# An encoder's gated MLP: the first contraction of 18 of 24 tile pairs by seven half products, the second in five pieces

## The chip, the cores and the metric

The kernel runs on one core of one Trainium2 chip. The metric is the device time of one execution in microseconds (us). Three runs of the kernel before took 1204.39, 1204.51 and 1204.84 us; their median is 1204.51 us.

## The reference

Two layers (L = 2) work on x of 512 tokens by 1024 features, in float32. Each layer has a mixing part (neighbourhood attention beside a recurrent branch) and a gated MLP; a last RMSNorm follows. The change works on the MLP:

```python
h = rmsnorm(x, g_ffn[l])
u = h @ w_up[l]                                  # 1024 -> 6144
u_act, u_lin = jnp.split(u, 2, axis=-1)
u_act = depthwise_conv(u_act, conv_ffn_w[l], conv_ffn_b[l], (1, 1))
x = x + (jax.nn.gelu(u_act, approximate=True) * u_lin) @ w_down[l]   # 3072 -> 1024
```

So tile j of the 24 tiles (128 features each) of `u_act` meets tile 24 + j of `u_lin`: these two are the *pair* j, and their product, tile j of h, is contracted with `w_down`.

## The kernel before, in words

Activations lie transposed: 128 features on the partitions, 512 tokens along the free axis. The tokens are stored in an order in which eight rows of a 64-wide grid alternate; `natural` and `by_row` (L350 on) are views that undo it for the convolution.

**Precision.** TensorE multiplies float32r values. Every operand is split into a high part (ScalarE copies to float32r) and a low part (VectorE subtracts), and `mm3` (L242 to L245) issues three matmuls per 128x128 block: high by high, high by low, low by high. All matmuls of the MLP but those at the very end have 512 columns, a whole PSUM bank.

**Weights.** `weight_plan` lists chunks of 128x1024 (eight blocks) in the order of their use. `load_to` (L170) starts their loads on SP's queue into two buffers `raw`, at most six chunks ahead; `split_to` (L190) makes the high and low part at most three chunks ahead (L157), on ScalarE (L205) and VectorE (L206), into four buffers each. `chunk` hands one out. The weights of layer 1's mixing are split during layer 0's MLP by `split_later` (L212): loads and stores of both parts on GpSimd's queue, the split at L222 and L223. In layer 1 they are loaded again as `kept`.

**MLP.** The first group (L866 to L873) computes pairs 0 and 1 in four banks, k by k, as the normalised inputs `xg` appear; before its k = 6 PE forms the sum of squares over the features (`columns`, tile `fcps`), before k = 7 it spreads the reciprocal root over the partitions (`rows`, tile `g_ffn_rb`). From then on each pair takes two columns of eight blocks (tiles `pa`, `pl`; L874 to L877), 48 matmuls. `mlp_tile` (L843 to L857) scales by `rbf`, does the three-tap convolution (L848 to L851), GELU on ScalarE (L853), the product with the linear tile (L854) and the split of h (L367, L368). After pairs 0 to 11 the second contraction takes its first twelve k blocks: four output tiles at once in four banks, then four one by one (tiles `dn`, L894 to L911); after pairs 12 to 23 the other twelve. `summed` (L882) scales the result and adds it to x. In layer 1 the last two output tiles are computed in token halves of 256 columns (`finish`, L435 to L506, tiles `dnf`), so that the final RMSNorm of the first half runs beside the products of the second.

**Order.** The framework orders each engine's instructions when the program is built; those emitted under `urgent()` (L151) go ahead of others that are ready. At run time each engine executes its list in order, and a waiting instruction holds all behind it.

## Time and profile before

| what | value |
|---|---|
| median of three runs | 1204.51 us |
| the profiled execution | 1204.35 us |
| span of its instructions | 1202.6 us |
| PE, weight loads, VectorE, ScalarE, GpSimd busy | 1188.4, 992.1, 752.9, 511.7, 114.0 us |
| mean granted clock of TensorE | 0.996 of full speed |
| layer 0: mixing, MLP | 0 to 204, 204 to 598 us |
| layer 1: mixing, MLP | 598 to 797, 797 to 1190 us |
| bytes over the DMA queues | 151.86 MB |

The profiled execution is 1.75 us longer than its span, and 0.16 us shorter than the median. Busy time is the time in which at least one instruction of that engine is executing: a matmul's record is longer than the step from one matmul to the next, so for PE the starts are read, not the durations.

### The profile page before, as it was taken

How to read it: one execution, taken by the hardware profiler on the slowest of the kernel's cores; microseconds unless marked ns; L12 is line 12 of the kernel's file. 1: busy time of each engine (PE TensorE's matmuls, PEld its weight loads, DVE VectorE, ACT ScalarE, POOL GpSimd, SP SyncE). 2: the span in 40 equal slices, each digit the busy share in tenths (PEclk: the TensorE clock that was granted, in tenths of full speed). 3: DMA queues.
4: the chain of work that ended last, by engine and by line, in shares of the span. 5: the costliest groups of instructions: out<-in, count | busy, mean ns of one | idle time of the engine just before them, and what ended most of it. 6: DMA issues, size and time to landing. Idle time of an engine off the chain costs nothing.

```text
span 1202.6 us, 14575 instructions
## 1 busy us (share of the span) xinstructions
PE 1188.4 (99%) x5534; PEld 992.1 (83%) x5534; DVE 752.9 (63%) x1226; ACT 511.7 (43%) x753; POOL 114.0 (9%) x230
## 2 busy tenths in 40 slices
PE   9999999999999999999999999999999999999996
PEld 8878888888888888888888888888888888888886
DVE  7988967776644567653736679587555336565443
ACT  6668854434321334422408578354233213333231
POOL 1102110123210122200002012000000000000000
PEclk9999999999999999999999999999999999999998
DMA  7222214376643376733256442232323232323222
GB/s 237 82 87 89 82 38 139 106 237 236 221 164 103 134 231 215 237 115 104 88 176 200 130 159 71 62 112 90 98 96 104 90 105 88 104 89 105 88 70 70
DMA packets 51046, 151.86 MB, mean 126 GB/s; under 512 B 6432, under 2 KB 9632, under 8 KB 50976
## 3 DMA queue, kind: packets, MB, share of 16 engines
q1 hardware_dynamic: 41792, 122.21, 31.1%
q0 software_dynamic: 8640, 28.32, 7.2%
q8 instruction: 43, 0.70, 0.2%
q10 hardware_dynamic: 544, 0.40, 0.1%
q14 instruction: 27, 0.22, 0.1%
HBM read 129.93 MB, written 20.97 MB: 125 GB/s over the span
## 4 chain that ended last, share of the span: by engine, by line
PE 91%; ACT 4%; DVE 3%; issue 1%; DVEq 0%; POOLq 0%; POOL 0%; ACTq 0%
PE dn L243 7%; PE dn L245 7%; PE dn L244 7%; PE pl L243 7%; PE pa L243 7%; PE pa L244 7%; PE pl L244 7%; PE pa L245 7%; PE pl L245 7%; PE out L245 2%; PE out L243 2%; PE out L244 2%; PE s L690 1%; PE xr L243 1%; PE up L243 1%; PE xr L244 1%
## 5 line engine op out<-in xcount | busy, mean ns | idle before, releaser
L205 ACT ACTIVATE hi<-raw 128x1024 fp32r<-128x1024 f32 (+1 forms) x189 | 197.6, 1046 | 380.5 <-PE dn L244 154.3
L206 DVE TENSOR_TENSOR lo<-raw,hi 128x1024 fp32r<-128x1024 f32 (+1 forms) x189 | 227.8, 1206 | 134.7 <-ACT hi L205 133.3
L845 DVE TENSOR_TENSOR ua<-pa,g_ffn_rb 128x512 f32<-128x512 f32 x44 | 30.4, 692 | 104.5 <-PE pa L245 104.5
L853 ACT ACTIVATE uc<-uc,cols 128x512 f32<-128x512 f32 x48 | 34.8, 724 | 116.2 <-DVE uc L851 116.1
L854 DVE TENSOR_TENSOR ua<-pl,uc 128x512 f32<-128x512 f32 x44 | 30.3, 689 | 45.0 <-PE pl L245 43.4
L467 POOL TENSOR_TENSOR fin_r<-fin_ms,expo 128x2 f32<-128x2 f32 x2 | 1.4, 696 | 377.0 <-DVE fin_ms L465 377.0
L851 DVE SCALAR_TENSOR_TENSOR uc<-ua,cols,uc 128x511 f32<-128x511 f32 x48 | 36.0, 751 | 1.6
L228 POOL DMA_DIRECT2D kept<-lhi x36 | 19.5, 542 | 182.1 <-ACT lhi L222 180.2
L849 DVE SCALAR_TENSOR_TENSOR uc<-ua,cols,uc 128x511 f32<-128x511 f32 x48 | 35.8, 746 | 0.1
L705 ACT ACTIVATE prob<-prob,mx 128x192 f32<-128x192 f32 (+1 forms) x64 | 27.5, 431 | 16.1 <-DVE mx L703 16.0
L223 DVE TENSOR_TENSOR llo<-lraw,lhi 128x512 fp32r<-128x512 f32 x36 | 24.7, 688 | 13.9 <-ACT lhi L222 13.9
L818 DVE TENSOR_TENSOR dns<-dn,g_ffn_rb 128x512 f32<-128x512 f32 x24 | 16.3, 689 | 24.8 <-PE dn L245 24.8
L222 ACT ACTIVATE lhi<-lraw 128x512 fp32r<-128x512 f32 x36 | 22.1, 616 | 8.0 <-DMA lraw<-in_w 8.0
L245 PE MATMUL out<-atth,lo 128*128 128x512 f32 x64 | 25.4, 397 | 0.0
L244 PE MATMUL out<-attl,hi 128*128 128x512 f32 x64 | 25.1, 394 | 0.0
L243 PE MATMUL out<-atth,hi 128*128 128x512 f32 x64 | 24.9, 402 | 0.0
L848 DVE TENSOR_SCALAR uc<-ua,cols 128x512 f32<-128x512 f32 x48 | 23.4, 488 | 1.5
L228 POOL DMA_DIRECT2D kept<-llo x36 | 19.5, 542 | 45.9 <-DVE llo L223 42.8
L690 PE MATMUL s<-k,q_pair 128*128 128x192 f32 (+1 forms) x128 | 22.7, 317 | 0.1
L640 POOL CAST edge<-vh 64x128 fp32r<-64x128 f32 x24 | 9.5, 394 | 120.3 <-ACT vh L627 55.9
L698 DVE CUSTOM_DVE_ANT_0 prob<-s,bias 128x192 f32<-128x192 f32 (+1 forms) x64 | 18.3, 337 | 3.9 <-PE s L690 3.6
L690 PEld LDWEIGHTS s<-k,q_pair 128*128 128x128 f32 x128 | 19.8, 190 | 1.0 <-DVE k L604 0.8
(935 smaller groups left out, 3633.6 us busy)
## 6 DMA issues: line engine op xcount, KB each, us to landing
raw<-in_w SPq DMA_DIRECT2D x183, 512.0 KB, 3.5
lraw<-in_w POOLq DMA_DIRECT2D x36, 256.0 KB, 4.6
kept<-lhi POOLq DMA_DIRECT2D x36, 256.0 KB, 2.5
kept<-llo POOLq DMA_DIRECT2D x36, 256.0 KB, 3.0
hi<-kept SPq DMA_DIRECT2D x36, 256.0 KB, 2.9
lo<-kept SPq DMA_DIRECT2D x36, 256.0 KB, 4.0
x<-in_x SPq DMA_DIRECT2D x8, 256.0 KB, 4.9
bias<-in_bias SPq DMA_DIRECT2D x8, 224.0 KB, 2.5
```

Of the source, the lines that this page charges most:

```text
L205: nc.scalar.activation(hi[:, sl], raw[:, sl], AF.Copy)
L206: nc.vector.tensor_tensor(out=lo[:, sl], in0=raw[:, sl], in1=f32(hi[:, sl]), op=ALU.subtract)
L228: nc.gpsimd.dma_start(d, f32(parts[h][n]))
L243: nc.tensor.matmul(ps, a[0], b[0], start=start, stop=False)
L244: nc.tensor.matmul(ps, a[0], b[1], start=False, stop=False)
L245: nc.tensor.matmul(ps, a[1], b[0], start=False, stop=stop)
L690: nc.tensor.matmul(ps[:, o:o + ROWS * w], q_pair[:, b], kt[:, ROWS * kc0:ROWS * (kc0 + w)], start=True, stop=True)
L845: nc.vector.tensor_tensor(out=by_row(ua), in0=natural(pa), in1=natural(rbf[0]), op=ALU.mult)
L849: nc.vector.scalar_tensor_tensor(out=c[:, 1:], in0=ua[:, :T - 1], scalar=w[0], in1=c[:, 1:], op0=ALU.mult, op1=ALU.add)
L851: nc.vector.scalar_tensor_tensor(out=c[:, :T - 1], in0=ua[:, 1:], scalar=w[2], in1=c[:, :T - 1], op0=ALU.mult, op1=ALU.add)
L853: nc.scalar.activation(c, c, AF.Gelu_apprx_tanh, bias=col("conv_ffn_b", j, l))
L854: nc.vector.tensor_tensor(out=natural(ua), in0=natural(pl_), in1=by_row(c), op=ALU.mult)
```

## The change

Only the MLP's pairs 6 to 23, the cut of the second contraction, the weight queue and some buffers change.

- **Seven products.** For a pair, split the contraction in two halves of four k blocks, the tokens in two halves of 256, and the outputs in their two tiles. Eight half products would give the pair; after sums of the weight halves and of the input halves, seven do. Each is 4 x 3 matmuls of 256 columns. Products 1, 6, 5, 3 accumulate in one bank, 7 and 4 in a second, 2 in a third; ScalarE copies the first bank after products 1, 6 and 5, and VectorE adds. `TURNS` orders the products of neighbouring pairs so that they alternate.
- **Weight sums.** `pair_sums` makes two summed chunks per pair on VectorE (four operations of 512), from up to six units ahead; the split then has 3.5 chunks per pair (parts a, b, c and the half part d) where there were two. Four `raw` buffers take the place of two; four new buffers `p_sum` hold the sums.
- **Inputs.** `operands` scales, sums and splits the inputs once per layer, for k = 0 to 3, during piece 0. Pairs 0 to 5 stay with eight products, in three groups.
- **After the products.** The linear tile is formed in halves, the convolution's first step moves to ScalarE, the scaling of the result falls away.
- **Second contraction** after pairs 0 to 5, 6 to 9, 10 to 13, 14 to 18 and 19 to 23.
- **Kept weights.** Only the low part is stored and reloaded, now on SP's queue; the high part is made again in layer 1. The zeroed tiles of the attention move into the `p_sum` buffers and are zeroed in each layer.

```diff
-HALF = NJ // 2
+PIECES = [0, 6, 10, 14, 19, NJ]
...
+FIRST_TURNS = [(0, 1), (0, 2), (1, 1), (0, 6), (1, 2), (0, 7), (0, 5), (1, 6), (0, 3), (1, 7), (0, 4), (1, 5)]
+TURNS = [(0, 1), (0, 2), (-1, 3), (0, 6), (0, 7), (-1, 4), (0, 5)]
+LAST_TURNS = [(0, 1), (0, 2), (-1, 3), (0, 6), (-1, 4), (0, 5), (0, 7), (0, 3)]
+PART = {1: ("a", 0), 2: ("a", 1), 6: ("b", 0), 7: ("b", 1), 5: ("c", 0), 3: ("c", 1), 4: ("d", 0)}
...
+    return [(j, m) for j in range(j0, j1) for m in range(4)] + [(j, m) for m in range(4, 8) for j in range(j0, j1)]
...
-    AHEAD_LOAD, AHEAD_SPLIT = 6, 3
+    AHEAD_LOAD, AHEAD_SUM, AHEAD_SPLIT = 7, 6, 3
...
+    def pair_sums(i):
+        a, b = raws[i], raws[i + 1]
+        s23 = p_sum.tile([P, 1024], F32, tag="sum", name=f"sb{i}")
+        s14 = p_sum.tile([P, 1024], F32, tag="sum", name=f"sc{i}")
+        lower, upper = slice(0, 512), slice(512, 1024)
+        for out, x0, x1, op in ((s14[:, lower], b[:, lower], b[:, upper], ALU.add),
+                                (s23[:, lower], s14[:, lower], a[:, lower], ALU.subtract),
+                                (s23[:, upper], a[:, lower], b[:, lower], ALU.subtract),
+                                (s14[:, upper], a[:, upper], s23[:, lower], ALU.subtract)):
+            with urgent(0):
+                nc.vector.tensor_tensor(out=out, in0=x0, in1=x1, op=op)
+        sums[i] = {"b": s23, "c": s14}
...
+                src = sums[i][part] if part in ("b", "c") else raws[i]
...
+    def split_later(split=True):
+        if not made:
+            if later:
+                i = later.pop(0)
+                raw = p_w2.tile([P, 1024], F32, tag="w2", name=f"lraw{i}")
+                nc.sync.dma_start(raw[:, 0:width(i)], w_d[i][:, 0:width(i)])
+                made.extend((i, raw))
...
+            kept[i] = p_kept.tile([P, width(i)], F32, tag=f"kept{i}", name=f"kept{i}")
+            nc.sync.dma_start(kept[i], raw[:, 0:width(i)])
+            made.clear()
...
-            nc.scalar.activation(probs_of[k // 4][:, k % 4], x[k][:, N:], AF.Copy, scale=col("g_final", k))
-        for m in (6, 7):
-            products(0, m, bank(0, m), 0, HALF)
-        ps = bank(1, 6)
-        products(1, 6, ps, 0, 5)
+        products(0, 6, bank(0, 6))
+        for k in range(5):
+            gained(k)
+        products(0, 7, bank(0, 7))
+        products(1, 6, bank(1, 6))
+        gained(5)
         r0 = columns(0)
-        products(1, 6, ps, 5, 9)
+        products(1, 7, bank(1, 7))
         rows(0, r0)
-        products(1, 6, ps, 9, HALF)
-        for k in range(6):
-            gained(k)
-        products(1, 7, bank(1, 7), 0, HALF)
         r1 = columns(1)
         for k in (6, 7):
             gained(k)
         rows(1, r1)
...
-            nc.vector.tensor_scalar(out=c, in0=ua, scalar1=w[1], scalar2=None, op0=ALU.mult)
+            nc.scalar.activation(c, ua, AF.Copy, scale=w[1])
...
+            for n in range(2):
+                cs = slice(n * N2, (n + 1) * N2)
+                nc.vector.tensor_tensor(out=natural(ua[:, cs]), in0=natural(lin[:, cs]), in1=by_row(c)[:, :, 4 * n:4 * n + 4],
+                                        op=ALU.mult)
+            hi = big(p_h, "h", f"h{l}_{j}h", F32R)
+            lo = big(p_h, "h", f"h{l}_{j}l", F32R)
+            behind(nc.scalar.activation(hi, ua, AF.Copy), first)
+            nc.vector.tensor_tensor(out=lo, in0=ua, in1=f32(hi), op=ALU.subtract)
...
+            for t, k_, src, dst in ((whole, k, low, low), (whole, k + 4, high, high),
+                                    (other, k, high, low), (other, k + 4, low, high)):
+                nc.vector.scalar_tensor_tensor(out=t[:, dst], in0=x[k_][:, src], scalar=col("g_ffn", k_, l),
+                                               in1=rbf[0][:, src], op0=ALU.mult, op1=ALU.mult)
+            s12 = big(p_t, "t", f"nc{l}{k}")
+            s34 = big(p_t, "t", f"nd{l}{k}")
+            for out, a, b in ((s12[:, low], other[:, low], whole[:, low]), (s12[:, high], whole[:, high], s12[:, low]),
+                              (s34[:, low], whole[:, high], other[:, low]), (s34[:, high], other[:, high], s12[:, high])):
+                nc.vector.tensor_tensor(out=out, in0=a, in1=b, op=ALU.subtract)
+            for src, at in ((whole, (1, 3)), (s12, (5, 6)), (s34, (7, 4))):
+                hi, lo = tile_of(f"oh{l}{k}{at[0]}"), tile_of(f"ol{l}{k}{at[0]}")
+                nc.scalar.activation(hi, src, AF.Copy)
+                nc.vector.tensor_tensor(out=lo, in0=src, in1=f32(hi), op=ALU.subtract)
+                for n, cs in zip(at, (low, high)):
+                    operand[n][k] = hi[:, cs], lo[:, cs]
+                if at[0] == 1:
+                    both = tile_of(f"o{l}{k}2")
+                    nc.scalar.activation(both[:, low], other[:, high], AF.Copy)
+                    nc.vector.tensor_tensor(out=both[:, high], in0=other[:, high], in1=f32(both[:, low]), op=ALU.subtract)
+                    operand[2][k] = both[:, low], both[:, high]
...
+        def turn(j, n):
+            c, half = take_part(j, n)
+            h = held.setdefault(j, {})
+            if n in (1, 7, 2):
+                pl = {1: ps_s, 7: ps_pt, 2: ps_o}[n]
+                h["ps", n] = psum(pl, f"up{l}{j}_{n}")[:, 0:N2]
+            ps = h["ps", {1: 1, 6: 1, 5: 1, 3: 1, 7: 7, 4: 7, 2: 2}[n]]
+            for k in range(4):
+                a = [t[:, (4 * half + k) * P:(4 * half + k + 1) * P] for t in c]
+                b = operand[n][k]
+                first = k == 0 and n in (1, 7, 2)
+                mm3(ps, a, b, first, k == 3, n in (6, 5, 3, 4))
...
+                with urgent():
+                    return nc.scalar.activation(h[name], ps, AF.Copy)
+            def added(out, a, b):
+                with urgent():
+                    nc.vector.tensor_tensor(out=out, in0=a, in1=b, op=ALU.add)
...
+            if n == 1:
+                settle("product", copy("u1"))
+            elif n == 6:
+                copy("u2")
+            elif n == 5:
+                settle("gelu", copy("u4"))
+                h["lin"] = big(p_t, "t", f"lin{l}{j}")
+            elif n == 2:
+                h["ua"] = big(p_t, "t", f"ua{l}{j}")
+                added(by_row(h["ua"])[:, :, 0:4], natural(h["u1"]), natural(ps))
+            elif n == 3:
+                with urgent():
+                    nc.scalar.activation(by_row(h["ua"])[:, :, 4:8], natural(ps), AF.Copy)
+                h["c"] = convolved(j, h["ua"])
+                if j + 1 not in PIECES:
+                    waiting["gelu"].append(lambda first, c=h["c"]: gated(j, c, first))
+                else:
+                    settle("product")
+                    gated(j, h["c"])
+            elif n == 4:
+                added(h["lin"][:, :N2], h["u2"], ps)
+                waiting["product"].append(lambda first, h=h: times_linear(j, h["ua"], h["c"], h["lin"], first))
+                if j + 1 in PIECES:
+                    settle("product")
+                del held[j]
+            if n in (5, 7) and "lin" in h and ("ps", 7) in h:
+                added(h["lin"][:, N2:], h["u4"], h["ps", 7])
...
+                    hooks = ({5: stats_columns, 7: stats_rows}, {4: lambda: operands(0)}, {2: lambda: operands(1)})[g]
+                    gemm_group(banks, "w_up", l, 0, 8, [2 * g, NJ + 2 * g, 2 * g + 1, NJ + 2 * g + 1], xn2.split, hooks)
...
+                for n, t in enumerate(turns(j0, j1)):
+                    turn(*t)
+                    if l == 0 and n % 3 == 2:
+                        split_later(n % 12 == 11)
...
-                    with urgent():
-                        nc.vector.tensor_tensor(out=x[m], in0=ps, in1=x[m], op=ALU.add)
-                else:
-                    add_scaled(m, ps, rbf[0], f"dns{l}{hf}{m}")
+                with urgent():
+                    nc.vector.tensor_tensor(out=x[m], in0=ps, in1=x[m], op=ALU.add)
...
+            for j in range(j0, j1):
+                for m in range(4):
+                    mm3(banks[m], down_blk(j, m), hs[j], j == j0, j == j1 - 1)
+                if j == j0 > 0:
+                    turn(j1 - 1, 4)
+                if j0 == 0 < j < 3:
+                    operands(j + 1)
+                if l == 0:
+                    split_later()
...
```

## Rows read from the trace of the kernel before

**Rows 1.** Windows by stage: us, then busy time of each engine, granted clock, DMA.
```profile
0.00:204.00 204.00, 200.99 (x989) 168.84 (x990) 164.70 (x343) 138.30 (x233) 28.33 (x67) 1.00 0.33 108
204.00:598.00 394.00, 394.00 (x1745) 326.50 (x1744) 238.13 (x315) 143.30 (x183) 60.70 (x109) 1.00 0.51 169
598.00:797.00 199.00, 198.53 (x981) 166.57 (x980) 132.76 (x285) 111.41 (x195) 21.60 (x51) 1.00 0.40 130
797.00:1190.00 393.00, 393.00 (x1814) 328.89 (x1812) 214.28 (x282) 117.86 (x142) 2.67 (x2) 1.00 0.29 93
```

**Rows 2.** The waits of PE, longest first: us in total, times, longest.
```profile
PE kps L243 <- DVE q_pair L596: 1.5, 1, 1.5
PE clock_ps L293 <- DVE ones L290: 1.0, 1, 1.0
```

**Rows 3.** Timeline of PE, last 512 and first 256 columns: start, duration in us.
```profile
1169.70 0.39 PE L243 MATMUL dn<-h_21h,hi 128*128 128x512 f32 x1
1171.74 0.28 PE L243 MATMUL dnf<-h_12h,hi 128*128 128x256 f32 x1
...
1180.37 0.28 PE L243 MATMUL dnf<-h_12h,hi 128*128 128x256 f32 x1
```

**Rows 4.** The stretch of 256 columns alone: its window, and one weight load of it.
```profile
1172.00:1182.00 10.00, 10.00 (x86) 10.00 (x85) 2.60 (x5) 1.87 (x4) 0.00 (x0) 1.00 0.01 2
...
L243 PEld LDWEIGHTS dnf<-h_13h,hi x4: 191/192/193, 1172.0 to 1186.0; 128*128 128x128 f32 x4
```

**Rows 5.** Groups of VectorE by line and shape: count, busy us, mean ns, idle before.
```profile
L206 DVE TENSOR_TENSOR lo<-raw,hi 128x1024 fp32r<-128x1024 f32 x183 | 223.8, 1223 | 130.5 <-ACT hi L205 129.1 <-DMA lo<-kept 0.9
L851 DVE SCALAR_TENSOR_TENSOR uc<-ua,cols,uc 128x511 f32<-128x511 f32 x48 | 36.0, 751 | 1.6
L854 DVE TENSOR_TENSOR ua<-pl,uc 128x512 f32<-128x512 f32 x44 | 30.3, 689 | 45.0 <-PE pl L245 43.4 <-ACT uc L853 1.6
L848 DVE TENSOR_SCALAR uc<-ua,cols 128x512 f32<-128x512 f32 x48 | 23.4, 488 | 1.5
L479 DVE SCALAR_TENSOR_TENSOR out<-x,cols,fin_rps 128x256 f32<-128x256 f32 x8 | 3.2, 475 | 1.6 <-PE fin_rps L474 1.6
L446 DVE TENSOR_TENSOR x<-dnf,x 128x256 f32<-128x256 f32 x4 | 1.7, 423 | 6.2 <-PE dnf L245 6.2
```

**Rows 6.** Timeline of VectorE in a dense stretch of a column pair.
```profile
445.72 0.68 DVE L854 TENSOR_TENSOR ua<-pl,uc 128x512 f32<-128x512 f32 x1
446.32 1.22 DVE L206 TENSOR_TENSOR lo<-raw,hi 128x1024 fp32r<-128x1024 f32 x1
447.45 0.68 DVE L368 TENSOR_TENSOR h_15l<-ua,h_15h 128x512 fp32r<-128x512 f32 x1
```

**Rows 7.** Groups of ScalarE by line and shape.
```profile
L205 ACT ACTIVATE hi<-raw 128x1024 fp32r<-128x1024 f32 x183 | 193.8, 1059 | 376.9 <-PE dn L244 154.3 <-PE pa L244 139.1 <-issue 27.0
L853 ACT ACTIVATE uc<-uc,cols 128x512 f32<-128x512 f32 x48 | 34.8, 724 | 116.2 <-DVE uc L851 116.1
L448 ACT ACTIVATE finsq<-x 128x256 f32<-128x256 f32 x4 | 1.7, 417 | 15.5 <-DVE x L446 15.5
```

**Rows 8.** Timelines of the first group, layers 0 and 1, around k = 5.
```profile
218.05 0.39 PE L243 MATMUL up<-xg_g_ffn_5h,hi 128*128 128x512 f32 x1
219.16 0.68 DVE L387 TENSOR_TENSOR g_ffn_acc<-g_ffn_acc,g_ffn_sq 128x512 f32<-128x512 f32 x1
...
808.55 0.39 PE L243 MATMUL up<-xg_g_ffn_5h,hi 128*128 128x512 f32 x1
809.65 0.69 DVE L387 TENSOR_TENSOR g_ffn_acc<-g_ffn_acc,g_ffn_sq 128x512 f32<-128x512 f32 x1
```

**Rows 9.** Timeline of the end: last product, last multiply by the norm.
```profile
1190.00 0.28 PE L245 MATMUL dnf<-h_23h,lo 128*128 128x256 f32 x1
...
1193.66 2.42 DVE L485 TENSOR_TENSOR prob<-prob,fin_rps 128x1024 f32<-128x1024 f32 x3 [1.55 <-PE fin_rps L474]
```

**Rows 10.** The DMA issues: KB each, median us to landing.
```profile
raw<-in_w SPq DMA_DIRECT2D x183, 512.0 KB, 3.5
```

More of the change, by code (lines that the diff above doesn't have):

```diff
@@ L190, in split_to @@
     def split_to(n):
-        while state["split"] < min(n, len(plan)):
-            i = state["split"]
-            if is_kept(i) and i > state["use"] + 2:
+        while state["split"] < min(n, len(units)):
+            u = state["split"]
+            what, _, part, (i, *_) = units[u]
+            if is_kept(i) and u > state["use"] + 2:
                 return
-            load_to(i + 1)
-            if i in kept:
-                halves[i] = highs.pop(i), lows.pop(i)
+            load_to(u + 1)
+            if i in lows:
+                hi = p_hi.tile([P, 1024], F32R, tag="hi", name=f"hi{i}")
+                sl = slice(0, width(i))
+                nc.scalar.activation(hi[:, sl], raws[i][:, sl], AF.Copy)
+                halves[u] = hi, lows.pop(i)
@@ L198, in split_to @@
                 state["split"] += 1
                 continue
-            raw = raws.pop(i)
-            hi = p_hi.tile([P, 1024], F32R, tag="hi", name=f"hi{i}")
-            lo = p_lo.tile([P, 1024], F32R, tag="lo", name=f"lo{i}")
+            part = part[1] if isinstance(part[1], str) else ""
+            if part in ("b", "c") and i not in sums:
+                pair_sums(i)
+            if part == "d":
+                src = raws[i + 1][:, 512:]
+                hi = big(p_fb, "fb", f"hi{i}d", F32R)
+                lo = big(p_fb, "fb", f"lo{i}d", F32R)
+                cuts = (slice(0, 512),)
+            else:
+                src = sums[i][part] if part in ("b", "c") else raws[i]
+                hi = p_hi.tile([P, 1024], F32R, tag="hi", name=f"hi{i}{part}")
+                lo = p_lo.tile([P, 1024], F32R, tag="lo", name=f"lo{i}{part}")
+                cuts = pieces(i)
@@ L236, in chunk, with mm3 @@
+    def chunk(w, l, first):
+        u = state["use"]
+        assert units[u][:3] == (w, l, first), (units[u], w, l, first)
+        split_to(u + 1 + AHEAD_SPLIT)
+        load_to(u + 1 + AHEAD_LOAD)
+        for _, _, part, chunks in units[u + 1 + AHEAD_SPLIT:u + 1 + AHEAD_SUM]:
+            if part[1] == "b" and chunks[0] not in sums:
+                pair_sums(chunks[0])
         state["use"] += 1
-        return halves.pop(i)
+        return halves.pop(u)
     def blk(c, i):
         return c[0][:, i * P:(i + 1) * P], c[1][:, i * P:(i + 1) * P]
-    def mm3(ps, a, b, start, stop):
-        nc.tensor.matmul(ps, a[0], b[0], start=start, stop=False)
-        nc.tensor.matmul(ps, a[0], b[1], start=False, stop=False)
-        nc.tensor.matmul(ps, a[1], b[0], start=False, stop=stop)
+    def mm3(ps, a, b, start, stop, more=False):
+        kw = {"skip_group_check": True} if more else {}
+        nc.tensor.matmul(ps, a[0], b[0], start=start, stop=False, **kw)
+        nc.tensor.matmul(ps, a[0], b[1], start=False, stop=False, **kw)
+        nc.tensor.matmul(ps, a[1], b[0], start=False, stop=stop, **kw)
@@ new lines, in convolved, with behind, gated, times_linear @@
+            return c
+        def behind(inst, first):
+            if first is not None:
+                tc.add_manual_dep(inst.ins, first.ins.name, BEHIND, reason="its wait must not hold up the other")
+        def gated(j, c, first=None):
+            behind(nc.scalar.activation(c, c, AF.Gelu_apprx_tanh, bias=col("conv_ffn_b", j, l)), first)
+        def times_linear(j, ua, c, lin, first=None):
+            for n in range(2):
[6 more added lines that the diff above has]
+            nc.vector.tensor_tensor(out=lo, in0=ua, in1=f32(hi), op=ALU.subtract)
+            hs[j] = hi, lo
@@ new lines, in operands, with tile_of @@
+        def operands(k):
+            def tile_of(name, dt=F32R):
+                taken[0] += 1
+                return big(p_h, "h", name, dt) if taken[0] <= 12 else big(p_xg, "xg", name, dt)
+            whole = big(p_t, "t", f"na{l}{k}")
+            other = big(p_t, "t", f"nb{l}{k}")
+            low, high = slice(0, N2), slice(N2, T)
+            for t, k_, src, dst in ((whole, k, low, low), (whole, k + 4, high, high),
[18 more added lines that the diff above has]
+                    operand[2][k] = both[:, low], both[:, high]
```

284 lines of the change are left out of this document (156 added, 128 removed).

## The prediction, made before the changed kernel was seen running

> **What bounds the kernel now.** I read the windows by stage first, to see which engine has no free time: in both MLP stages PE is busy for the whole of it (394.00 of 394.00 us, 393.00 of 393.00), VectorE for 238.13 and 214.28 us, ScalarE for 143.30 and 117.86 [rows 1]. Then the waits of PE: the longest of the whole run is 1.5 us, and neither of the first two lies in the MLP [rows 2]. So in the MLP a matmul removed is time gained, until another engine has less left than PE. VectorE is the next in line, and the change loads it.
>
> A busy PE says nothing of its pace; the starts in its timeline do. Nine matmuls of 512 columns lie between 1169.70 and 1171.74: 0.2267 us each. Seventy-two of 256 columns lie between 1171.74 and 1180.37: 0.1199 each [rows 3]. The granted clock is 1.00 in that stretch, the 2.4 GHz level [rows 4]. Half the columns thus cost 53%, not 50%.
>
> **PE, the gain.** A pair takes 48 matmuls of 512 now, 48 x 0.2267 = 10.88 us. After: 7 products x 4 blocks x 3 = 84 of 256, 84 x 0.1199 = 10.07 us. Per pair 0.81 us, for 18 pairs in 2 layers 29.2 us. An eighth product less would be 12.5%; the narrower matmul takes back 5 points.
>
> The weight load is the doubt here. In the stretch of 256 columns each load takes 192 ns, more than the step, and the loads are busy for 10.00 of 10.00 us, yet the step is 120 ns [rows 4]: loads overlap one another there. The Trainium skill (TensorE: Matmul & The Clock Gate, Back-to-back issue gap) gives for streams of load and matmul about 81 ns at 128 columns and 131 ns at 512, an interpolated 98 ns at 256 being my estimate from that page; by it 84 x 98 ns against 48 x 131 ns would cost 1.9 us more per pair, 70 us slower in all. The rows disagree with both of its levels, and the sum goes by the rows.
>
> The second contraction has the same matmuls in other pieces. At the very end 144 matmuls of 256 become 60 of 256 and 42 of 512: 17.27 against 7.19 + 9.52 us, a gain of 0.6 us. PE in all: -29.8 us.
>
> **VectorE, per pair.** Durations come from the groups [rows 5]: 1024 elements 1.22 us, 512 elements 0.69, 256 elements 0.42, a convolution step 0.75. Before: two splits of weights, scale, first tap 0.49, two taps, product, split of h: 6.5 us in 8 operations. After: four sums 2.76, splits of 3.5 chunks 4.36, three additions of 256 1.27, two taps 1.50, product in halves 0.85, split of h 0.69: 11.4 us in 16 operations. But back to back VectorE starts the next one sooner: 0.60 us after one of 512, 1.13 after one of 1024 [rows 6], some 0.085 us below the duration; dense, the pair costs 11.4 - 16 x 0.085 = 10.1 us, and before 6.5 - 8 x 0.085 = 5.8. PE's pair is 10.07: in a row of products VectorE would just keep up. Beside the second contraction (24 x 0.2267 = 5.44 us of PE per tile) it needs only one split of weights and about 1.8 additions of 512, 2.4 us, so over a whole piece it has room: four pairs cost it 4 x (10.1 + 2.2) = 49 us dense of PE's 62. The look-ahead (three splits and two pairs of sums, 9 us) moves part of the surplus into the contraction before.
>
> Per layer `operands` comes on top, beside piece 0: 4 x 6.1 us (four scalings of 256 at 0.475, four subtractions, three splits of 512 and one of 256), 5.1 each when dense. With 18 x 4.3 us for the pairs, 20 for these and some 5 for eight more additions, VectorE goes from 238 to 340 us in layer 0 and from 214 to 316 in layer 1 [rows 1], 90% and 83% of the 379 that PE keeps. The kept weights cost it 36 splits as before. The nearest stage to that is layer 0's mixing: 164.70 of 204 us, 81%, with the 1.5 us wait among PE's few [rows 1, 2]. So VectorE does not bound as a whole, and it is late at places.
>
> **What comes back, place by place.**
> - *The sum of squares moves from k = 6 to k = 5.* PE reaches k = 5 at 218.05 and 808.55; the accumulator is finished at 219.16 + 0.68 = 219.84 and 809.65 + 0.69 = 810.34 [rows 8]. PE waits 1.8 us in each layer, the matmuls of k = 5 to 7 queued behind it: I take 3.6 us (0 if VectorE's list comes out with the accumulator earlier, 3.6 otherwise).
> - *Piece 0 into the first products.* Beside its second contraction (32.6 us) VectorE has the end of pairs 4 and 5, half of `operands`, splits, sums for the first two pairs and eight additions, 35 to 39 us. Late by 0 to 6 us per layer; the first product needs only the inputs, so I take 1.5, in all 3.
> - *The copies between products.* Each bank is copied by ScalarE before the next product accumulates in it. Where two products lie between (2.88 us), a copy of 0.42 behind one operation of up to 1.06 [rows 7] is hidden. In the first and last turns of a piece three copies have one product (1.44 us): latency, 0.42 and a full operation ahead exceed it by some 0.3 us. 24 such places, 0 to 0.4 us each; 0.1 taken: 2.4.
> - *The end of a piece.* After product 3 of its last pair, the copy, three convolution steps, GELU, product and split follow one another: 0.42 + 0.72 + 1.50 + 0.72 + 0.85 + 0.72 + 0.69 = 5.6 us with nothing in the way, while PE has three tiles and product 4, 9.6 us, in a piece of four. Seven hand-overs, each behind what VectorE or ScalarE is doing: 0 to 2 us for each of 8 pieces; 0.4 taken: 3.2.
> - *The end of the kernel.* The last half product now takes 1.8 us instead of 4.3, so the first half's eight final multiplies (0.39 us apart when dense) fall into the 3.7 us between the last product and the last multiply [rows 9], where VectorE is mostly waiting. -1 to +3.3; 1 taken.
> - *Layer 1's mixing* makes 20 high parts on ScalarE, about 19 us on 111.41: below the 138.30 that layer 0's mixing carries without cost [rows 1]. Zeroing the tiles on GpSimd, hidden by the second contraction before. 0, either up to 1.
> - *SP's queue* takes the kept weights over from GpSimd's: a store that waits for VectorE holds up the weight loads behind it. The loads run up to seven units ahead and land 3.5 us after issue [rows 10]: hidden; without that cover one late load costs PE what is left of the 3.5 us.
>
> Sum, against the profiled execution's 1204.35: -29.8 + 3.6 + 3 + 2.4 + 3.2 + 1 = -16.6, which gives 1187.8. The median of the runs, 1204.51, is 0.16 us above; I say **1188**.
>
> **The rivals.**
> - *All hidden.* The waits above vanish in the look-ahead; only the end costs its 1 us: 1204.35 - 29.8 + 1 = 1175.6. For: VectorE's 81% with PE unharmed. Against: the wait for the sum of squares, which nothing hides [rows 8]. 0.15.
> - *Slower: VectorE bounds the rows of products.* If its 16 operations can't run dense, because each pair of split and copy waits for ScalarE, the pair costs its durations, 11.4 us, against 10.07: 36 x 1.33 = 47.9, so 1175.6 + 47.9 = 1223.5 where the look-ahead catches nothing, about 1211 where it catches a quarter. It decides from 10.07 + 0.81 = 10.88 us per pair on. For: VectorE spends 130.5 us before its weight splits waiting now, 129.1 of them for ScalarE [rows 5]. Against: those waits fell where it had nothing else to do. The Trainium skill (VectorE: DVE Perf Modes, The TRN2 errata) advises tiles of at least 512 elements, since the latency of an operation is paid once each; the trace agrees, two of 256 taking 0.85 and one of 512 0.69. 0.12.
> - *The second weight chunk comes late.* Its `raw` buffer is free only when part d of the pair two before is split. Split, landing, sums and the split of b are 0.7 + 3.5 + 2.8 + 2.3 = 9.3 us; PE passes the units between in 7 to 15 us, according to how early the split ran. Half a microsecond per pair would make 18: 1188 + 9 to 18, 1197 to 1206. 0.10.
> - *Loads that don't overlap* in the new products: the load's 0.192 us sets the step, 84 x 0.192 = 16.1 us per pair, 189 us more, 1393. [rows 4] show the same kind of matmul at 0.12. 0.01. The Trainium skill's section named above would have narrow matmuls slow for the same reason.
>
> **How the numbers follow.** My forecast (1180 to 1197) has 0.62. A measurement of this kernel can tell 0.2%, 2.4 us. Faster: the forecast, all hidden, and most of the late chunk, 0.62 + 0.15 + 0.07 = 0.84. The same: 0.03 from the late chunk. Slower: 0.12 + 0.01 = 0.13. The range goes from 1175, all hidden, to 1204, the late chunk at nearly its full price; left out are the slower cases and the edge of the hidden one, 0.17.
>
> **What the profile after would show.** Right: starts of products 0.120 us apart, a pair's seven in 10.1 us; PE's waits of some 1.8 us at `fcps`, some tenths at the copies `u`, a few at h of a piece's last tile; VectorE at 80 to 90% of the MLP stages. Wrong: waits for the sums or the low parts of w_up in each pair (VectorE bounds), waits of ScalarE's copy of weights for the load (late chunk), or PE without gaps (all hidden).

## The result, and the profile after

The changed kernel takes **1177.28 us** (median of 4 runs, 1176.57 to 1177.69) against 1204.67 (1204.39 to 1204.92) before on the same chip: a ratio of 0.9772, 95% interval 0.9755 to 0.9789. It gains 27.4 us; 16.5 were forecast. The profiled execution takes 1177.09 us, its span is 1175.3.

The busy time of each engine after, from the page:

```profile
PE 1160.8 (99%) x6788; PEld 1028.8 (88%) x6788; DVE 950.1 (81%) x1634; ACT 679.4 (58%) x1069; POOL 56.5 (5%) x130
```

The windows by stage after answer to [rows 1], with the same columns; they are layer 0's MLP, layer 1's mixing and layer 1's MLP:

```profile
204.00:584.30 380.30, 380.23 (x2393) 345.66 (x2392) 332.84 (x516) 215.36 (x326) 4.77 (x9) 1.00 0.42 141
584.30:782.30 198.00, 196.99 (x974) 165.37 (x973) 135.27 (x288) 130.01 (x217) 21.00 (x51) 1.00 0.44 146
782.30:1162.00 379.70, 378.51 (x2409) 344.90 (x2407) 310.44 (x476) 194.37 (x291) 1.01 (x1) 1.00 0.29 91
```

VectorE has gone from 238.13 to 332.84 us and from 214.28 to 310.44, 88% and 82% of its stages, and PE still has hardly a gap: 380.23 of 380.30, 378.51 of 379.70. The waits of PE, longest first, answer to [rows 2] (us in total, times, longest):

```profile
PE kps L323 <- DVE q_pair L677: 1.5, 1, 1.5
PE clock_ps L373 <- DVE ones L370: 1.0, 1, 1.0
...
PE dn L324 <- DVE h_13l L947: 0.7, 1, 0.7
PE dn L324 <- DVE h_9l L947: 0.5, 1, 0.5
```

The two longest stood there before. The change brings two waits into the MLP that the list names: for the low part of h of the last tile of a piece, tiles 9 and 13 in layer 1, 1.2 us in all.

Where the gain lies, from the starts of the first matmul of each stage in the two traces:

| stage | before, us | after, us | difference |
|---|---|---|---|
| up to the first `up` of layer 0 | 204.45 | 204.90 | +0.45 |
| MLP, layer 0, to the first `xr` | 393.11 | 379.42 | -13.69 |
| mixing, layer 1, to the first `up` | 197.39 | 197.96 | +0.57 |
| MLP, layer 1, to the last `dnf` | 395.05 | 381.86 | -13.19 |
| last `dnf` to the end of the span | 12.60 | 11.16 | -1.44 |

PE's count in the prediction was 18 x 0.81 = 14.6 us in layer 0 and 15.2 in layer 1. So 0.9 and 2.0 us came back within the MLPs, where 13.2 were forecast for the whole kernel. (In the kernel before, layer 1's MLP begins at 794.95, where its first `up` runs; the 797 of the table and of [rows 1] is a rounder bound.)

The starts of the first row of products answer to [rows 3]. Timeline of PE after: the last matmul of piece 0's contraction, the first of the products, the first of the next contraction.

```profile
304.02 0.39 PE L325 MATMUL dn<-h_5h,lo 128*128 128x512 f32 x1
304.25 0.28 PE L323 MATMUL up<-oh,hi50a 128*128 128x256 f32 x1
...
343.61 0.40 PE L323 MATMUL dn<-h_6h,hi 128*128 128x512 f32 x1
```

Twenty-seven products of twelve matmuls lie between 304.25 and 343.61, 39.36 us; at 0.1199 each they need 38.85. The first product follows the contraction by 0.23 us, one step of 512 columns: nothing waited. Half a microsecond is all that this row of products loses, 0.33 of it at one copy of a bank (310.72 to 311.41).

How close that was shows in the windows of piece 0's contraction, layer 0 and layer 1:

```profile
271.60:304.25 32.65, 32.65 (x145) 27.04 (x144) 32.48 (x59) 16.42 (x24) 0.00 (x0) 1.00 0.30 99
849.00:881.60 32.60, 32.60 (x145) 27.04 (x144) 32.54 (x58) 14.83 (x21) 0.00 (x0) 1.00 0.21 66
```

VectorE works through the whole of it, 32.48 of 32.65 us and 32.54 of 32.60, and PE loses nothing. There the margin is used up, and further on a margin is left.

### The profile page after: what moved, and what is told of

The parts are those of the page before. It is cut to its first block, busy times and chain, and to the rows that moved or that the text cites. A ratio compares the mean times of both kernels' runs of the same rounds, so it can differ in the third digit from the quotient of the medians.

```text
span 1175.3 us, 17693 instructions
## 1 busy us (share of the span) xinstructions
PE 1160.8 (99%) x6788; PEld 1028.8 (88%) x6788; DVE 950.1 (81%) x1634; ACT 679.4 (58%) x1069; POOL 56.5 (5%) x130
## 4 chain that ended last, share of the span: by engine, by line
PE 67%; DVE 3%; DMA 2%; ACT 1%; issue 0%; DVEq 0%; ACTq 0%
PE up L323 11%; PE up L324 11%; PE up L325 11%; PE dn L324 6%; PE dn L325 6%; PE dn L323 6%; DMA raw<-in_w 2%; PE out L325 1%; PE out L323 1%; PE out L324 1%; DVE lo L273 1%; PE s L771 1%; PE kps L323 1%; PE xr L323 1%; PE kps L325 1%; PE xr L325 1%
## 5 line engine op out<-in xcount | busy, mean ns | idle before, releaser
L273 DVE TENSOR_TENSOR lo<-raw,hi 128x1024 fp32r<-128x1024 f32 (+1 forms) x117 | 139.9, 1198 | 37.8 <-ACT hi L272 36.8
L272 ACT ACTIVATE hi<-raw 128x1024 fp32r<-128x1024 f32 (+1 forms) x117 | 120.8, 1033 | 77.0 <-PE up L324 24.7
L1026 ACT ACTIVATE u<-up 128x256 f32<-128x256 f32 x108 | 40.9, 380 | 67.4 <-PE up L325 67.4
L1093 DVE TENSOR_TENSOR x<-dn,x 128x512 f32<-128x512 f32 x78 | 51.3, 684 | 18.4 <-PE dn L325 18.3
L942 DVE TENSOR_TENSOR ua<-lin,uc 128x256 f32<-128x256 f32 x96 | 36.6, 419 | 12.3 <-ACT uc L936 12.3
L923 ACT ACTIVATE uc<-ua,cols 128x512 f32<-128x512 f32 x48 | 34.6, 721 | 16.1 <-DVE ua L955 15.1
L253 ACT ACTIVATE hi<-raw 128x1024 fp32r<-128x1024 f32 (+1 forms) x20 | 19.4, 972 | 22.9 <-issue 5.6
L1030 DVE TENSOR_TENSOR lin<-u,up 128x256 f32<-128x256 f32 x72 | 29.9, 415 | 1.3 <-ACT u L1026 0.8
L240 DVE TENSOR_TENSOR sc<-raw 128x512 f32<-128x512 f32 x36 | 24.7, 687 | 7.5 <-DMA raw<-in_w 7.2
L240 DVE TENSOR_TENSOR sb<-sc,raw 128x512 f32<-128x512 f32 x36 | 24.7, 687 | 0.5
L240 DVE TENSOR_TENSOR sc<-raw,sb 128x512 f32<-128x512 f32 x36 | 24.6, 684 | 0.0
```

The costliest lines, as they stand in the source:

```text
L240: nc.vector.tensor_tensor(out=out, in0=x0, in1=x1, op=op)
L272: nc.scalar.activation(hi[:, sl], src[:, sl], AF.Copy)
L273: nc.vector.tensor_tensor(out=lo[:, sl], in0=src[:, sl], in1=f32(hi[:, sl]), op=ALU.subtract)
L942: nc.vector.tensor_tensor(out=natural(ua[:, cs]), in0=natural(lin[:, cs]), in1=by_row(c)[:, :, 4 * n:4 * n + 4], op=ALU.mult)
L1026: return nc.scalar.activation(h[name], ps, AF.Copy)
L1093: nc.vector.tensor_tensor(out=x[m], in0=ps, in1=x[m], op=ALU.add)
```

## The experiments

Eleven runs were made of ten kernels, in three batches. Those of one batch stand beside runs of the kernel before on the same chip: 1204.74 (`eight_half`, `sums_plus2`, `sums_plus4`, `four_plain`), 1204.39 (`hook3`, `one_between`, `no_ahead`, `pieces_of_six`) and 1204.45, the median of 7 (the last three). The first eight are single runs; the theory was by then that VectorE keeps up because the list of its instructions lets it run ahead beside the contractions, and the rival that single waits were luckily hidden and VectorE is at the brink everywhere.

**PE's term: `eight_half`.** The kernel before, with pairs 6 to 23 computed in half products, but all eight of them and without any sums:

```diff
+    def halved_column(ps, w, l, m, rhs):
+        c = chunk(w, l, (0, m))
+        for th in range(2):
+            cs = slice(th * 256, th * 256 + 256)
+            for k in range(8):
+                mm3(ps[:, cs], blk(c, k), [a[:, cs] for a in rhs[k]], k == 0, k == 7)
...
+                    column = gemm_column if j < 6 else halved_column
-                    gemm_column(pa, "w_up", l, j, xg2)
+                    column(pa, "w_up", l, j, xg2)
-                    gemm_column(pl_, "w_up", l, NJ + j, xg2)
+                    column(pl_, "w_up", l, NJ + j, xg2)
```

> The kernel before, with the columns of pairs 6 to 23 computed as eight half products of 256 columns (96 matmuls per pair in place of 48 of 512), nothing else changed. Theory (the step per matmul is all that counts, 0.1199 us at 256 columns): 36 x (96 x 0.1199 - 10.88) = +22.7 us, near 1227 us. Rival (narrow matmuls are slower where weights change with every one, as loads of 192 ns might): well above 1227, up to 36 x (96 x 0.192 - 10.88) = +272 us.

1227.89 us, 23.15 more than before; 36 x (96 x 0.1199 - 10.88) = 22.7 was the count. Halving the matmuls costs what the step says, so the gain of the change is 22.7 us paid for the narrower matmul and 52 us taken back by the eighth product (36 x 12 x 0.1199).

**Room on VectorE: `sums_plus2` and `sums_plus4`.** The first sum of each pair is made three times, and five times: two and four more operations of 512 elements, 1.2 and 2.4 us per pair when dense.

```diff
             with urgent(0):
-                nc.vector.tensor_tensor(out=out, in0=x0, in1=x1, op=op)
+                for _ in range(1 + (2 if op == ALU.add else 0)):
+                    nc.vector.tensor_tensor(out=out, in0=x0, in1=x1, op=op)
```

> The changed kernel with one of the four weight sums of each pair computed three times instead of once: two more VectorE operations of 512, 1.2 us dense per pair, 43 us in all. Theory A (VectorE has room over a whole piece and its list and the look-ahead spread it): 1177 to 1181 us. Theory B (a row of products is bound by VectorE as soon as a pair costs it more than PE's 10.07 us): 10.1 + 1.2 against 10.07, up to 36 x 1.2 = 43 us more, some 1195 to 1220 us.

> As the run before with four more operations, 2.4 us dense per pair, 86 us in all. VectorE was busy for 333 of 380 us in layer 0's MLP and 310 of 380 in layer 1's, so 376 and 353 then. Theory A: room ends here in layer 0, 1185 to 1200 us. Theory B: up to 86 us more, 1230 to 1263 us.

1181.58 and 1199.03, 4.3 and 21.8 us above the changed kernel: theory A in the second; the first lies 0.6 us above the edge of its theory A and far below theory B. VectorE's pair then takes 10.1 + 1.2 = 11.3 and 12.5 us beside PE's 10.07. If the rows of products had to wait for it, 36 x 1.2 = 43 and 36 x 2.4 = 87 us would be due; a tenth and a quarter of that came. VectorE makes up the rest beside the contractions. The bend lies between: the first 1.2 us per pair cost 0.12 us each on average, the next 1.2 cost 0.49. It is an average and not a price of every pair: `sums_plus2` loses 3.5 us at the first products behind piece 0 of layer 0 (1.4 of them at a lower clock, see the end) and 2.5 at the ends of the next two pieces there, while its layer 1's MLP takes 381.21 us, 0.65 less than in the changed kernel.

The windows of the MLP stages of `sums_plus4` show how full it is then, layer 0 first:

```profile
204.80:604.30 399.50, 388.20 (x2389) 350.36 (x2388) 370.02 (x584) 212.97 (x326) 4.76 (x9) 0.99 0.42 134
802.30:1186.10 383.80, 381.72 (x2426) 347.15 (x2425) 349.17 (x550) 194.54 (x293) 1.87 (x2) 1.00 0.29 90
```

At 93% and 91% PE is idle for 11.3 and 2.1 us; at 88% and 82% in the changed kernel for 0.1 and 1.2. Some 4.4 us more of the 21.8 are steps at a lower granted clock, 47 of them in three stretches of layer 0 (see the end).

VectorE's share alone does not explain why layer 0 loses so much more than layer 1 at nearly the same share. The weights to be kept are made in layer 0 only, and the largest wait of PE there, 2.8 us for a copy of a bank, goes back to them: the copy stood on ScalarE behind the split of a kept weight, which waited 6.18 us for its load. From the list of PE's waits and the timeline of ScalarE in `sums_plus4`:

```profile
PE up L324 <- ACT u L1027: 4.8, 4, 2.8
```

```profile
377.74 1.15 ACT L298 ACTIVATE lhi<-lraw 128x512 fp32r<-128x512 f32 x2 [6.18 <-DMA lraw<-in_w]
378.79 0.36 ACT L1027 ACTIVATE u<-up 128x256 f32<-128x256 f32 x1
```

How much of layer 0's price is due to these loads is not shown; no run leaves the kept weights out.

**Two pairs more in seven products: `four_plain` and `four_no_ahead`.** Piece 0 with four pairs in two groups, so that 20 pairs of a layer have seven products; `operands` moves up. PE alone would gain 2 x 2 x 0.81 = 3.2 us.

```diff
-PIECES = [0, 6, 10, 14, 19, NJ]
+PIECES = [0, 4, 9, 14, 19, NJ]
...
-                for g in range(3):
-                    pls = ((ps_mm, ps_mm, ps_mm, ps_s), (ps_s, ps_pt, ps_pt, ps_mm), (ps_mm, ps_mm, ps_s, ps_s))[g]
+                for g in range(2):
+                    pls = ((ps_mm, ps_mm, ps_mm, ps_s), (ps_s, ps_pt, ps_pt, ps_mm))[g]
...
-                    hooks = ({5: stats_columns, 7: stats_rows}, {4: lambda: operands(0)}, {2: lambda: operands(1)})[g]
+                    hooks = ({5: stats_columns, 7: stats_rows}, {2: lambda: operands(0), 6: lambda: operands(1)})[g]
```

> The changed kernel with only pairs 0 to 3 by eight products (pieces of 4, 5, 5, 5, 5 pairs; two groups instead of three). PE's work falls by 2 x 2 x 0.81 = 3.2 us. Theory A (PE bounds every stage): 1174 us. Theory C (beside the first piece VectorE is at its limit, busy 32.5 of 32.7 us in its second contraction now): 65 us of PE against some 70 of VectorE there, 1178 to 1190 us, with PE waiting for inputs or weights ahead of the first seven-product pair.

1182.70, 5.4 us more than the changed kernel: theory C. The longest wait of PE in `four_plain`, and the windows before and of the stretch behind it:

```profile
PE up L325 <- DVE lo46a L273: 3.0, 1, 3.0
```

```profile
271.60:279.00 7.40, 4.31 (x31) 3.70 (x30) 7.40 (x15) 3.68 (x7) 0.00 (x0) 1.00 0.19 79
279.00:285.60 6.60, 5.93 (x26) 5.44 (x27) 6.60 (x9) 3.15 (x6) 0.00 (x0) 0.51 0.58 174
```

VectorE is busy for all of both stretches and PE waits for it: the low part of the second pair's first chunk is late. For the first products behind piece 0 the prediction had set 1.5 us per layer; with two tiles less in piece 0 it is more than that. It also costs twice, since the granted clock is 0.51 in the 6.60 us behind the wait (more on that below).

`four_no_ahead` is the same with the sums of coming pairs asked for later, so that VectorE need not make them there.

```diff
-    AHEAD_LOAD, AHEAD_SUM, AHEAD_SPLIT = 7, 6, 3
+    AHEAD_LOAD, AHEAD_SUM, AHEAD_SPLIT = 7, 3, 3
```

> Four tiles without the products, as in four_plain, with sums asked for three units ahead. Theory A (VectorE beside piece 0's second contraction was too full by the sums of coming pairs, some 2.8 us each, two pairs): the wait of 3.0 us for the low part at the first products goes, and with PE's two pairs less in halves (2 layers x 2 pairs x 0.81 = 3.2 us) the time is 1171 to 1176. Rival B (operands alone and the end of pairs overfill VectorE there, and the sums that are needed first come late instead): 1178 to 1186, with a wait for a low part or for a sum's split in layer 0.

1181.51 (median of 4 runs; ratio 0.9811, 0.9794 to 0.9827): rival B. Two of its three longest waits of PE lie at that place (the third is the old one for `q_pair`):

```profile
PE up L325 <- DVE lo46a L273: 1.5, 1, 1.5
...
PE up L323 <- ACT hi44b L272: 1.5, 1, 1.5
```

The late low part loses half of its wait, and the sums that were put off are late in its place: `hi44b` is the high part of a summed chunk. So sums made ahead are not by themselves what overfills VectorE beside a shorter piece 0. The work of `operands`, the largest that is left there, is the likely cause, but no run takes it out alone. Of the two cuts tried, six pairs and four, four are too few.

**The sum of squares: `hook3`.** It is asked for two blocks earlier, before k = 3.

```diff
-                    hooks = ({5: stats_columns, 7: stats_rows}, {4: lambda: operands(0)}, {2: lambda: operands(1)})[g]
+                    hooks = ({3: stats_columns, 7: stats_rows}, {4: lambda: operands(0)}, {2: lambda: operands(1)})[g]
```

> The changed kernel with the sum of squares over the features asked for ahead of k = 3 of the first group instead of k = 5. Theory A (the framework lists an instruction of PE where its operands are ready, so the matmuls of the group go ahead of it): unchanged, within 1 us of 1177. Rival, my step (PE stands at that place until the accumulator is finished): PE would reach k = 3 some 7 us ahead of it in each layer, +14 us, 1191 us.

1177.92, no difference. Where `fcps` runs, in the timeline of PE of the changed kernel and then of `hook3`:

```profile
220.54 0.39 PE L323 MATMUL up<-xg_g_ffn_5h,hi 128*128 128x512 f32 x1
220.76 0.95 PE L459 MATMUL fcps<-ones,g_ffn_acc 128*128 128x1 f32 x8
221.57 0.49 PE L324 MATMUL up<-xg_g_ffn_5l,hi 128*128 128x512 f32 x1
```

```profile
220.51 0.94 PE L459 MATMUL fcps<-ones,g_ffn_acc 128*128 128x1 f32 x8
221.32 0.49 PE L324 MATMUL up<-xg_g_ffn_5l,hi 128*128 128x512 f32 x1
```

Asked for ahead of k = 5 in the changed kernel and of k = 3 in `hook3`, it runs at the same point, with ten of the twelve matmuls of k = 5 ahead of it, half a microsecond after its accumulator is done (219.61 + 0.69 = 220.30 in the changed kernel). In the kernel before, asked for ahead of k = 6, it ran at 220.77. So PE's instructions are not listed in the order in which the kernel asks for them, and here the sum was listed about where its data were ready.

**The copies between products: `one_between`.** Each pair is worked alone, so that between a product and the next in its bank lies one other, or none (6 and 5 of a piece's first pair).

```diff
-FIRST_TURNS = [(0, 1), (0, 2), (1, 1), (0, 6), (1, 2), (0, 7), (0, 5), (1, 6), (0, 3), (1, 7), (0, 4), (1, 5)]
-TURNS = [(0, 1), (0, 2), (-1, 3), (0, 6), (0, 7), (-1, 4), (0, 5)]
-LAST_TURNS = [(0, 1), (0, 2), (-1, 3), (0, 6), (-1, 4), (0, 5), (0, 7), (0, 3)]
+FIRST_TURNS = [(0, 1), (0, 2), (0, 6), (0, 5), (0, 7), (0, 3)]
+TURNS = [(0, 1), (0, 2), (0, 6), (-1, 4), (0, 5), (0, 7), (0, 3)]
+LAST_TURNS = TURNS
...
-    for j in range(j0 + 2, j1):
+    for j in range(j0 + 1, j1):
...
-            if part[1] == "b" and chunks[0] not in sums:
+            if part[1] == "b" and chunks[0] not in sums and chunks[0] + 1 in raws:
```

The last line is a second change: where the load of a pair's second chunk has not been issued, the sums are made a unit later.

> The changed kernel with another order of products: every copy of a bank by ScalarE has one other product (1.44 us) before the next product accumulates in that bank, instead of two mostly; in the first pair of each piece the copy after product 6 has none. (Sums are made a unit later where the load had not been issued.) Theory A (1.44 us covers copy and hand-over): only the 8 places with none cost, some 0.8 us each, 1182 to 1185 us. Rival, my step (0.1 to 0.4 us for each place with one product): some 80 more such places, 8 to 32 us on top, 1190 to 1215 us.

1179.26, 2.0 us more, below what either theory expected. All gaps over 0.06 us between matmuls of the MLPs (what a step has beyond 0.1199 or 0.2267 us) add up to 4.9 us there against 2.7 in the changed kernel, where 1.5 are the two waits for h. These waits are not there in `one_between`, which the later sums may explain (see `no_ahead`). So the order of products by itself costs more than 2.0 us: the gaps at copies add up to 3.9 us against 0.5. In the first row of products a copy's place loses at most 0.3 us, mostly 0.15 before the first matmul behind the copy and 0.10 before the second. Ahead of it stands part of another product that the turns ask for later (eleven matmuls of one, the product behind the copy, then the twelfth); nothing is listed as a wait.

**The look-ahead of the sums: `no_ahead`, `no_ahead_timed`.** A unit is one of the parts a to d of a pair's weights, or one chunk elsewhere. Sums are asked for three units ahead, no sooner than the splits, in place of six (the edit shown for `four_no_ahead`, made to the changed kernel alone).

> The changed kernel with the weight sums asked for three units ahead, when the split needs them, not six. Theory A (the look-ahead of the sums carries VectorE's surplus from the rows of products into the second contractions): some 5 us per piece come back into the rows, VectorE late there, 1180 to 1200 us. Rival (the list orders them by readiness anyway and the buffers set the pace): within 1.5 us of 1177.

1175.01, 2.3 us less than the changed kernel, where theory A had 3 to 23 us more and the rival at most 1.5 less: neither held. The two waits for h are gone. Timeline of VectorE in layer 1 at the end of piece 1, in the changed kernel:

```profile
928.16 0.69 DVE L240 TENSOR_TENSOR sc<-raw 128x512 f32<-128x512 f32 x1 [0.21 <-DMA raw<-in_w]
928.77 0.68 DVE L240 TENSOR_TENSOR sb<-raw,raw 128x512 f32<-128x512 f32 x1
929.37 1.22 DVE L273 TENSOR_TENSOR lo166a<-raw,hi166a 128x1024 fp32r<-128x1024 f32 x1
930.50 0.69 DVE L947 TENSOR_TENSOR h_9l<-ua,h_9h 128x512 fp32r<-128x512 f32 x1
```

and in `no_ahead_timed`:

```profile
927.41 0.69 DVE L240 TENSOR_TENSOR sc<-raw 128x512 f32<-128x512 f32 x1
928.01 0.69 DVE L947 TENSOR_TENSOR h_9l<-ua,h_9h 128x512 fp32r<-128x512 f32 x1
928.62 1.22 DVE L273 TENSOR_TENSOR lo166a<-raw,hi166a 128x1024 fp32r<-128x1024 f32 x1
```

With the look-ahead, two sums (0.21 us of waiting for their load in front of them) and a split of weights stand between the last product's work and the low part that PE needs next; without it, one sum stands there and h_9l comes 2.5 us sooner (0.5 of them because this layer's MLP starts that much earlier). ScalarE has a part in it: with the look-ahead the high part h_9h, which h_9l needs, stands behind a split of weights and starts at 928.38, without it at 926.78. Which ends of pieces wait depends on the whole list: `hook3`, with the same look-ahead, waits for h at four of them, 1.7 us as listed, and `pieces_of_six` below at none. The same kernel was run again:

> The same kernel as no_ahead (sums asked for three units ahead in place of six), timed in rounds. Theory A (the sums asked for early are listed on VectorE ahead of the last low part of a piece, and that costs): 1174.0 to 1176.5, below the changed kernel's 1177.28, since the one run gave 1175.01. Rival B (2.3 us was the spread of single runs): 1176.6 to 1178.

**1174.77 us** (median of 4 runs, 1174.37 to 1175.21; ratio 0.9754, 0.9739 to 0.9768): theory A. The intervals of the two ratios overlap; the runs (1176.57 to 1177.69 and 1174.37 to 1175.21, each beside its own chip's 1204.67 and 1204.45) do not. It is the fastest kernel here, ahead of the changed one by 2.5 us and of the one before by 29.7. The gaps over 0.06 us in both MLPs together are 0.6 us against 2.7.

**Fewer pieces: `pieces_of_six` and `six_no_ahead`.** Four pieces of six pairs, with the look-ahead and without.

```diff
-PIECES = [0, 6, 10, 14, 19, NJ]
+PIECES = [0, 6, 12, 18, NJ]
```

> The changed kernel with four pieces of six pairs instead of five of 6, 4, 4, 5, 5: eight additions fewer per layer, but six pairs of products in a row between two second contractions. Theory A (VectorE needs what PE needs in a row, and the look-ahead covers the rest): 1176 to 1179 us. Theory B (a surplus builds up over a row): PE waits grow with the length of the row, 1182 to 1200 us.

> Four pieces of six tiles with sums asked for three units ahead. Theory A (the two edits act on the same waits, at the ends of pieces): 1174 to 1177, as no_ahead alone; with one piece less, two of its ends fall away, at most 0.6 us each. Rival B (in longer rows of products VectorE, at 10.1 us a pair against 10.07, falls further behind, and without sums made ahead it shows): 1179 to 1185 with waits for sums' splits late in the rows.

1178.29 and 1177.33 (median of 4 runs, 1176.14 to 1177.97; ratio 0.9774, 0.9759 to 0.9789). Rows of six pairs where there were four or five don't let VectorE fall behind: neither trace lists a wait for the split of a sum in them, so rival B falls in both. Theory A holds for the first and misses the second by 0.3 us. The two MLPs together take 759.5 and 759.1 us, as much as the 759.1 of `no_ahead_timed` and less than the 761.3 of the changed kernel. In both the longest new wait is outside the MLP, in layer 1's mixing, here in `pieces_of_six`:

```profile
PE gp L323 <- ACT ti L645: 1.9, 1, 1.9
```

In `six_no_ahead` it is 1.6 us, most of the 2.6 that separate it from `no_ahead_timed`. Why another cut of the MLP makes this stage wait was not tried.

## Why the prediction was right or wrong

Faster was right, and 1177.28 lies in the range near its lower end; the forecast was 10.7 us too slow. "All hidden", 1175.6 with a chance of 0.15, came closest. The gain on PE was right and the price of the waits was not: 13.2 us were set, 2.5 came in all (29.8 less the 27.3 by which the span shrank).

- **PE, -29.8: right.** The row of 27 products keeps the step of [rows 3], and `eight_half` gives 23.15 us where the same step gives 22.7. The rule of the Trainium skill that was weighed (TensorE: Matmul & The Clock Gate, Back-to-back issue gap), by which narrow matmuls behind their loads would have made the change 70 us slower, fails here; the trace has 0.120 us at 256 columns.
- **VectorE's total: right.** 340 and 316 us were worked out, 332.84 and 310.44 are there.
- **"PE waits 1.8 us in each layer" at `fcps`, 3.6: failed.** The step mistook the place where the kernel asks for the sum for the place where PE runs it. PE ran it at 220.76, where it had run before, and `hook3` shows that an even earlier request costs nothing. The prediction's own bound, 0 if the list comes out otherwise, was the value.
- **Piece 0 into the first products, 3: mis-sized, it is 0.** VectorE's 35 to 39 us were to fit in 32.6; the windows have it full for 32.5, and what was over must have been done earlier or later. `four_plain` shows that the mechanism is real, with 3.0 us once piece 0 is shorter, and so does `sums_plus2` with 1.2 us at this place.
- **The copies with one product between, 2.4: mis-sized.** 0.33 and 0.18 us at two places in layer 0's first row of products, no gap over 0.06 us at any other copy. The first is not a matter of distance: the product to be copied had ended some 5 us before. ScalarE's list has four splits of weights ahead of the copy, and the last of them waited 1.28 us for the load of a kept weight:

```profile
310.11 0.63 ACT L297 ACTIVATE lhi<-lraw 128x512 fp32r<-128x512 f32 x1 [1.28 <-DMA lraw<-in_w]
310.65 0.64 ACT L1026 ACTIVATE u<-up 128x256 f32<-128x256 f32 x2
```

  `one_between` has some 80 more such places for 3.4 us, since PE's list fills the distance with other products.
- **The end of a piece, 3.2: the mechanism right, the size not.** Two of eight places wait, 1.2 us as listed, 1.5 as gaps. What makes them is not the chain of 5.6 us by itself but the work listed among it, the early sums above all. The prediction's sentence that "the look-ahead ... moves part of the surplus into the contraction before" thus has the wrong sign at this place: without it the waits vanish, and `no_ahead_timed` gains 2.5 us.
- **The end of the kernel, +1: wrong sign for the whole of it.** The timeline of the end after answers to [rows 9]:

```profile
1164.14 0.28 PE L325 MATMUL dnf<-h_23h,lo 128*128 128x256 f32 x1
...
1166.10 2.43 DVE L546 SCALAR_TENSOR_TENSOR out<-x,cols,fin_rps 128x256 f32<-128x256 f32 x6
...
1168.45 2.41 DVE L552 TENSOR_TENSOR out_of<-out_of,fin_rps 128x1024 f32<-128x1024 f32 x3
```

  The six multiplies of the first half do stand in front of the last ones, which begin 4.31 us after the last product instead of 3.66: the step was right with +0.65 (the diff also reorders the instructions of the close). But from the start of the last multiplies to the end of the span are 6.85 us instead of 8.94. The prediction has no term for this. The difference is the drain with which GpSimd's queue ends (count, shortest/median/longest in ns, first and last start), before and after:

```profile
L983 POOLq DRAIN  x3: 40/93/9642, 1192.2 to 1202.3; - x3
L1202 POOLq DRAIN  x3: 40/82/802, 1166.2 to 1175.0; - x3
```

  Before, it takes 9.64 us from 1192.15 on and ends at 1201.80, 2.0 us after SP's queue is done; after, it takes 0.80 us and is over long before. `eight_half`, whose kept weights still use GpSimd's queue, has 9.65 us, and every kernel with the change has 0.80. That the moved transfers are the reason, and not another of the changes to GpSimd's work, is argued: no run moves them alone.
- **SP's queue and layer 1's mixing, 0: right within its bound.** The mixing takes 197.96 us against 197.39, 0.6 more where up to 1 was allowed. Of the queue, one late load of a kept weight shows, in the 0.33 us above.

Of the rivals, VectorE as the bound of the rows of products was said to decide "from 10.07 + 0.81 = 10.88 us per pair on". `sums_plus2` stands at 11.3 us dense and loses 0.12 us per pair on average; `sums_plus4` at 12.5 and loses 0.61. The point was set as if each row of products stood alone. The late second chunk shows as VectorE's wait before the first sum of a pair, and hardly reaches PE. The group of VectorE after that bears on it (count, busy us, mean ns, idle before), beside [rows 5]:

```profile
L240 DVE TENSOR_TENSOR sc<-raw 128x512 f32<-128x512 f32 x36 | 24.7, 687 | 7.5 <-DMA raw<-in_w 7.2
```

VectorE waits 7.2 us for the load over 36 pairs, 0.2 us each; at 928.16 above, such a wait stands in front of the one for h_9l. Of the copies, the 108 of tile `u` wait 67.4 us in all for PE; the other way round it is the tenths named above.

What is left open: of the 2.0 us that came back in layer 1's MLP, 1.5 are the gaps at the two waits, 0.2 the steps right behind them, and some 0.4 lie in fractions of a thousandth of a microsecond per step, with no gap to name.

## What to carry to other kernels

A stage is judged by whether its second engine has room over the stage, and each local lateness only after asking what the list of instructions can put in its place: here two of four local prices came to nothing and the other two to half or less, and VectorE kept up at 88% of a stage, while at 91 to 93% PE was idle for 2 us in one layer and 11 in the other. Where the order of instructions is made by a framework, the place of an operation is read from the trace, not from the line that asks for it. And a look-ahead is work put in front of something: on the engine that is nearly full, ask what it stands ahead of.

## What the runs showed of the hardware that was not expected

**A short wait can cost twice.** In `sums_plus2` PE waits 1.2 us for a low part and 0.3 for a copy; half a microsecond behind the second, its steps of 256 columns nearly double. The timeline of PE there:

```profile
309.79 0.28 PE L325 MATMUL up<-ol,hi52b 128*128 128x256 f32 x1
311.26 0.38 PE L326 MATMUL up<-oh,lo52b 128*128 128x256 f32 x1 [1.20 <-DVE lo52b L274]
...
312.44 0.41 PE L324 MATMUL up<-oh,hi50b 128*128 128x256 f32 x1
312.65 0.42 PE L325 MATMUL up<-ol,hi50b 128*128 128x256 f32 x1
...
315.82 0.28 PE L325 MATMUL up<-o,hi52a 128*128 128x256 f32 x1
```

and the windows before, of and behind the slow stretch:

```profile
309.00:312.40 3.40, 1.91 (x13) 1.50 (x13) 2.96 (x5) 1.93 (x5) 0.00 (x0) 0.99 0.56 166
312.45:315.60 3.15, 3.15 (x16) 3.15 (x16) 2.63 (x5) 1.40 (x3) 0.00 (x0) 0.50 0.80 226
316.00:319.00 3.00, 3.00 (x27) 3.00 (x27) 2.39 (x4) 1.45 (x2) 0.00 (x0) 1.00 0.53 137
```

The granted clock is 0.50, the 1.2 GHz level, for some 3 us, with steps of 0.213 us instead of 0.120, and 1.00 again behind it. Fifteen matmuls at 0.093 us more are 1.4 us, as much as the waits themselves. In `four_plain`, behind 3.0 us of waiting, the clock is 0.51 for 6.6 us. The two waits of the changed kernel, 0.5 and 0.7 us as listed, have no such stretch behind them, and neither has a wait of 1.2 us (for lo150a, up to 861.3) in layer 1 of `four_plain`, where the window behind it has a granted clock of 1.00:

```profile
861.50:865.00 3.50, 3.20 (x26) 3.00 (x26) 3.50 (x6) 1.40 (x2) 0.00 (x0) 1.00 0.00 0
```

So the length of one wait does not settle it in these runs. And the 4.3 us of `sums_plus2` and the 5.4 of `four_plain` are not all waiting.
